# Low parts of weights made a layer ahead, memory values as split products, and a planner that goes backwards and forwards

## The chip, the cores and the metric

The kernel runs on one core of one Trainium2 chip. The metric is the device time of one execution in microseconds (us), smaller is better; a median of several runs is compared. A profile is one execution taken by the hardware profiler: it lists each instruction of TensorE (PE for its matmuls, PEld for its weight loads), VectorE (DVE), ScalarE (ACT), GpSimd (POOL), and SyncE (SP), which only issues DMAs here. GpSimd issues DMAs too, on a queue of its own.

## The reference

One inference step of a two-layer streaming encoder, in fp32, for 384 tokens of width 1024: 8 running streams of 16 tokens (128) and one new stream of 256. Layer 0 mixes tokens by a Conformer convolution, layer 1 by a gated deltanet:

```python
h = rms_norm(x, P['norm_pre'][i, 0])
f = swiglu(h, ...);  x = x + 0.5 * rms_norm(f, P['norm_post'][i, 0])
h = rms_norm(x, P['norm_pre'][i, 1])
y = conformer_conv_module(h, ...) if i % 2 == 0 else gated_deltanet(h, ...)
x = x + rms_norm(y, P['norm_post'][i, 1])
h = rms_norm(x, P['norm_pre'][i, 2])
a = memory_cross_attention(h, mem_k[i], mem_v[i], ...)
x = x + rms_norm(a, P['norm_post'][i, 2])
h = rms_norm(x, P['norm_pre'][i, 3])
f = swiglu(h, ...);  x = x + 0.5 * rms_norm(f, P['norm_post'][i, 3])
```

`swiglu` is `(silu(h @ w_gate) * (h @ w_up)) @ w_down` with an inner width of 2816. The convolution module is a 1024 to 2048 projection, a gate (`val * sigmoid(gate)`), a depthwise convolution of 31 taps, a layer norm with silu, and a 1024 to 1024 projection with bias. For the new stream, memory keys and values are outputs, and needed by the cross-attention of each layer:

```python
p_mem_k = jnp.einsum('bmd,lde->lbme', mem_prompt, xa_wk)   # 256 memory tokens, 2 layers
p_mem_v = jnp.einsum('bmd,lde->lbme', mem_prompt, xa_wv)
```

The running streams bring theirs in a cache.

## The kernel before

**Split products.** An fp32 weight chunk of 128 x 1024 numbers (512 KB) is loaded into one of three `raw` buffers (SP), cast by ScalarE to a rounded type, fp32r, as its high part `whi`, and DVE subtracts to get the low part `wlo` (`Emitter.get`, L289 and after; the subtraction is L197's, the cast L189's). High and low parts lie in a ring of eight buffers each: chunk j takes buffer j % 8, and `done` frees it in the program's order. Activations are split likewise (`hTh`, `hTl`; `rbh`, `rbl`). A product is then three fp32r matmuls: high x high, high x low, low x high. All matmuls are issued at L247 (`mm`), transposes at L279.

**Kinds of products.** `gmm` makes 128 output features for all 384 tokens: 8 k-steps x 3 matmuls of 384 columns. `dmm` adds one k-step of a down projection: for 128 tokens and each half of 512 output columns 3 matmuls. `wide` is a projection of 512 features with tokens as rows.

**Stages in order.** Start (three norm chains), feed-forward block of layer 0 (`ffn(0, 0)`), convolution (`conv`), cross-attention (`xattn(0)`), feed-forward (`ffn(0, 1)`), then for layer 1 feed-forward, `deltanet`, `xattn(1)`, feed-forward. A feed-forward block has 22 passes f: a gate chunk, an up chunk, and the down chunk of an earlier pass, so 48 matmuls of 384 columns and 18 of 512. At the end of each stage `tokenwise` finishes three groups of 128 tokens in turn, each followed by a `chain`: the sum of squares on ScalarE, a power on GpSimd (`rstd`), the residual on DVE, transposes, and the next split.

**The convolution.** Eight pairs of input chunks (`cg`, `cv`); each pair's result is gated (`glu`: GpSimd clears the left padding, ScalarE and DVE make the product and copy a window). DVE then applies 31 taps per feature chunk (`taps`, L210), two chunks at a time; taps that meet only cached rows are done in the block before (`old_taps`). PE adds up the mean, `ln` normalises on DVE, ScalarE, PE and GpSimd, and eight output chunks (`co`, all eight weight buffers) with a bias chunk (`bout`, split into spare columns of `rbh` and `rbl`) finish it.

**Memory keys and values.** `kv(n)` emits n units, taken from a list: for both kinds, 2 layers, 4 heads and 2 feature halves, 32 units in all. A unit loads 512 KB of weights as plain fp32 into a slot (four slots beside the memory itself, in `big`), does 16 fp32 matmuls of 128 columns, copies the result on ScalarE, and GpSimd stores it. The units have no successors in their stage, so they fill PE's idle time; the table `KV` says how many are emitted where (start 3, first block 3, convolution 20, its output 3, then 1 and 2).

**What sets the order.** The program is emitted once into a list of operations, each with a cost from a formula (`act`, `tt`, `ts`, `mm`, ...). `Scheduler.graph` finds dependencies from the parts of the tiles that are read and written. `Scheduler.order` then simulates: each of the five engines takes, whenever it is free, the ready operation with the longest path of costs to the end, plus a bonus given by hand. DMAs go through one pipe of 360 bytes per ns, eight in flight per queue. The instructions of each engine are issued in the order found, and each engine works strictly through its own.

## Time and profile before

| | us |
|---|---|
| median of 3 runs | 1885.33 |
| lowest and highest | 1884.56, 1886.7 |
| the profiled execution | 1886.81 |
| its span, first to last instruction | 1885.0 |

The profiled execution had a granted clock of 0.999. About 1.8 us of its time lies around its span. "Busy" counts an engine's instructions alone; a DMA's time to landing runs from its issue to the arrival of its last byte.

### The profile page before, as it was taken

The numbers are of one execution on the slowest core, as the hardware profiler recorded it, in microseconds if no ns is written. First come the engines' busy times: TensorE is split into PE (matmuls) and PEld (weight loads), VectorE is DVE, ScalarE is ACT, GpSimd is POOL, SyncE is SP. The second block draws the span as 40 slices with busy tenths as digits, with TensorE's granted clock in tenths as the row PEclk, the third lists the DMA queues.
The fourth block names the chain that finished last, engine by engine and source line by source line (L and its number), as shares of the span: only waits on it lengthen the run. The fifth ranks groups of instructions, "written<-read, shape, count | busy, mean of one in ns | idle before, by whom it ended". The sixth has DMA issues, their size and how long they took to land.

```text
span 1885.0 us, 27534 instructions
## 1 busy us (share of the span) xinstructions
PE 1860.1 (99%) x10895; PEld 1682.0 (89%) x10895; DVE 1011.6 (54%) x1708; ACT 753.8 (40%) x1435; POOL 170.2 (9%) x391
## 2 busy tenths in 40 slices
PE   8999999999999999999999999999999999999998
PEld 8999999999877899999899999999998766899997
DVE  6564436999553633333633333688776734533333
ACT  4333334312643632333433233676564534432332
POOL 1000002111100100000100000323221101000000
PEclk9999999999999999999999999999999999999999
DMA  8543434556686534434434333323325682444331
GB/s 303 178 136 126 134 112 122 127 147 219 213 314 216 157 123 134 132 125 130 154 115 131 123 124 111 118 79 116 126 93 165 228 316 74 137 132 135 123 123 45
DMA packets 88466, 278.81 MB, mean 148 GB/s; under 512 B 18001, under 2 KB 20561, under 8 KB 88337
## 3 DMA queue, kind: packets, MB, share of 16 engines
q1 hardware_dynamic: 86080, 271.42, 44.8%
q0 software_dynamic: 2256, 5.64, 0.9%
q8 instruction: 85, 1.39, 0.3%
q14 instruction: 45, 0.36, 0.1%
HBM read 265.09 MB, written 11.92 MB: 147 GB/s over the span
## 4 chain that ended last, share of the span: by engine, by line
PE 94%; DVE 1%; DMA 1%; ACT 1%; POOL 1%; issue 1%; SPq 0%; DVEq 0%; POOLq 0%; ACTq 0%
PE ps L247 89%; PE ps L279 3%; PE ps L259 2%; POOL stat L197 1%; DVE big L210 1%; ACT big L190 1%; DMA big<-in_cv 0%; DMA x<-in_x 0%; DMA raw<-in_w 0%; PE ps L272 0%; DVE big L197 0%; ACT hTl L190 0%; ACT whi L189 0%; DMA big<-in_state 0%; DVE wlo L197 0%
## 5 line engine op out<-in xcount | busy, mean ns | idle before, releaser
L197 DVE TENSOR_TENSOR wlo<-raw,whi 128x1024 fp32r<-128x1024 f32 x361 | 438.6, 1222 | 581.4 <-ACT whi L189 555.7
L189 ACT CAST whi<-raw 128x1024 fp32r<-128x1024 f32 x361 | 374.5, 1051 | 652.5 <-PE ps L247 603.5
L247 PE MATMUL ps<-hTh,wlo 128*128 128x384 f32 x1680 | 495.4, 339 | 0.0
L247 PE MATMUL ps<-hTh,whi 128*128 128x384 f32 (+1 forms) x1680 | 494.5, 340 | 0.1
L247 PE MATMUL ps<-hTl,whi 128*128 128x384 f32 x1680 | 493.8, 340 | 0.0
L247 PEld LDWEIGHTS ps<-hTh,whi 128*128 128x128 f32 x1680 | 308.7, 188 | 8.0 <-ACT big L190 1.0
L247 PEld LDWEIGHTS ps<-hTl,whi 128*128 128x128 f32 x1680 | 308.8, 188 | 6.9 <-issue 1.5
L247 PEld LDWEIGHTS ps<-hTh,wlo 128*128 128x128 f32 x1680 | 309.0, 188 | 4.2 <-issue 0.4
L247 PE MATMUL ps<-big 128*128 128x128 f32 (+3 forms) x1912 | 283.7, 286 | 9.9 <-DMA big<-in_w 6.4
L247 PEld LDWEIGHTS ps<-big 128*128 128x128 f32 x1912 | 256.7, 193 | 35.0 <-issue 17.8
L247 PE MATMUL ps<-whi,rbh 128*128 128x512 f32 x672 | 205.2, 396 | 0.4 <-DVE big L210 0.4
L247 PE MATMUL ps<-wlo,rbh 128*128 128x512 f32 x672 | 203.0, 395 | 0.0
L247 PE MATMUL ps<-whi,rbl 128*128 128x512 f32 x672 | 201.7, 394 | 0.0
L210 DVE SCALAR_TENSOR_TENSOR big<-big,cols 128x384 f32<-128x384 f32 (+13 forms) x424 | 189.3, 499 | 2.6 <-ACT big L190 0.3
L247 PEld LDWEIGHTS ps<-whi,rbl 128*128 128x128 f32 x672 | 125.7, 188 | 24.8 <-issue 0.4
L247 PEld LDWEIGHTS ps<-wlo,rbh 128*128 128x128 f32 x672 | 125.3, 188 | 24.6 <-issue 0.8
L247 PEld LDWEIGHTS ps<-whi,rbh 128*128 128x128 f32 x672 | 124.9, 188 | 20.5 <-DVE big L210 0.6
L279 PE MATMUL ps<-ident,big 128*128 128x128 f32 x479 | 86.0, 275 | 6.0 <-DVE big L210 5.6
L247 PE MATMUL ps<-whi,hTh 128*128 128x512 f32 x240 | 87.7, 401 | 0.2 <-ACT hTh L189 0.2
L197 DVE TENSOR_TENSOR big<-big,ps 128x384 f32<-128x384 f32 (+4 forms) x131 | 67.2, 519 | 36.2 <-PE ps L247 36.1
L247 PE MATMUL ps<-whi,hTl 128*128 128x512 f32 x240 | 86.4, 398 | 0.1
L204 POOL TENSOR_SCALAR stat<-stat 128x1 f32<-128x1 f32 (+2 forms) x48 | 16.8, 350 | 767.6 <-ACT hTl L190 754.0
(84 smaller groups left out, 1337.8 us busy)
## 6 DMA issues: line engine op xcount, KB each, us to landing
raw<-in_w SPq DMA_DIRECT2D x362, 512.0 KB, 3.7
big<-in_w SPq DMA_DIRECT2D x37, 512.0 KB, 4.7
big<-in_ck SPq DMA_DIRECT2D x32, 512.0 KB, 6.3
big<-in_cv SPq DMA_DIRECT2D x32, 512.0 KB, 6.6
big<-in_npre SPq DMA_DIRECT2D x8, 512.0 KB, 7.5
big<-in_npost SPq DMA_DIRECT2D x8, 512.0 KB, 6.2
out_pkv<-big POOLq DMA_DIRECT2D x32, 128.0 KB, 5.1
big<-out_pkv SPq DMA_DIRECT2D x8, 512.0 KB, 6.3
```

The source lines that it names most:

```text
L189: return self._on("A", cost, dep, lambda: sc.copy(out, in_), [in_], w)
L190: return self._on("A", cost, dep, lambda: sc.activation(out, in_, func, **kw), [in_, bias, scale] + ([] if after is None else [after]), w, ...
L197: return self._on(eng, cost, dep, lambda: e.tensor_tensor(out=out, in0=a, in1=b, op=op), [a, b], [out])
L204: return self._on(eng, cost, dep, lambda: e.tensor_scalar(out=out, in0=a, scalar1=s1, scalar2=s2, op0=op0, **kw), [a, s1, s2 if s2 is not ...
L210: lambda: v.scalar_tensor_tensor(out=out, in0=a, scalar=s, in1=b, op0=op0, op1=op1), [a, s, b], [out])
L247: self._add("P", cost, lambda: t.matmul(out, lhsT, rhs, start=start, stop=stop, **kw), [lhsT, rhs], [out])
L259: t.matmul(out, lhsT, rhs, start=start, stop=stop)
L279: self._add("P", 109.0, lambda: t.transpose(out, in_, ident), [in_, ident], [out])
```

## The change

**Values as split products.** The value weights become 16 chunks `("v4", layer, half of 512 columns, quarter of k)`. A new function, emitted after the convolution's input chunks, splits the memory (two chunks, into columns of `rbh` and `rbl` that the bias does not use) and multiplies; the list of `kv` keeps the 16 key units, each now 8 fp32 matmuls of 256 columns:

```diff
+    def kv_split(self):
...
+        for i in range(2):
+            c = slice(i * D, (i + 1) * D)
+            E.get(("mem", i), dest=(mh[:, c], ml[:, c]))
...
+        for l in range(2):
+            for u in range(2):
+
+                (o, b) = self.bank2()
+                for q in range(4):
+                    j, wh, wl = E.get(("v4", l, u, q))
+                    for k in range(2 * q, 2 * q + 2):
+                        s = slice(512 * (k % 2), 512 * (k % 2) + 512)
+                        for m in range(2):
+                            c = slice(m * P, (m + 1) * P)
+                            E.mm(o[m], mh[:, k, c], wh[:, s], k == 0, False)
+                            E.mm(o[m], mh[:, k, c], wl[:, s], False, False)
+                            E.mm(o[m], ml[:, k, c], wh[:, s], False, k == KT - 1)
+                            E.pump()
+                    E.done(j)
+                for m in range(2):
+                    r = result(o[m], 512)
+                    for n in range(2):
+                        E.store(self.O["pkv"][l, 2 * u + n][:, 512 + m * MEM:512 + (m + 1) * MEM],
+                                r[:, n * MEM:(n + 1) * MEM])
...
-            for m in range(2):
-                c = slice(m * P, (m + 1) * P)
-                for k in range(KT):
-                    a, b_ = (w[:, k, :], mem[:, k, c]) if kind == "wk" else (mem[:, k, c], w[:, k, :])
-                    E.mm(o[:, c], a, b_, k == 0, k == KT - 1)
+            for k in range(KT):
+                E.mm(o[:, 0:MEM], w[:, k, :], mem[:, k, :], k == 0, k == KT - 1)
...
-KV = {"start": 3, "f00": 3, "conv": 20, "co": 3, "xo": 0, "f01": 1, "f10": 2, "dn": 6, "f11": 0}
+KV = {"start": 3, "f00": 3, "conv": 5, "co": 2, "xo": 0, "f01": 1, "f10": 2, "dn": 0, "f11": 0}
-SLOTS = 4
+SLOTS = 3
```

**Low parts made ahead.** 35 chunks, those of the convolution's last four input pairs, the memory, the values, the bias and the output projection, are split once more than needed, two in each pass f = 3 to 20 of the first feed-forward block: loaded, cast, subtracted, and the low part stored in DRAM by GpSimd. When the chunk is needed, its high part is made as before, and its low part is loaded by GpSimd's queue into the weight buffer; the subtraction goes.

```diff
+AHEAD = [(n, k) for k in range(4, KT) for n in ("cg", "cv")] + [("mem", 0), ("mem", 1)]
+AHEAD += [("v4", l, u, q) for l in range(2) for u in range(2) for q in range(4)] + [("bout",)] + [("co", k) for k in range(KT)]
...
         self.load(raw, self.wall[CHUNK[name]])
         self.act(hi, raw)
-        self.tt(lo, raw, hi.bitcast(F32), ALU.subtract)
+        if name in self.low:
+            self.store(lo, self.low.pop(name))
+        else:
+            self.tt(lo, raw, hi.bitcast(F32), ALU.subtract)
         return j, hi, lo
+
+    def ahead(self, name):
+
+        j, hi, lo = self.get(name)
+        self.low[name] = self.scr[self.nlow]
+        self.nlow += 1
+        self.store(self.low[name], lo)
+        self.done(j)
...
+            if (l, i) == (0, 0) and f >= FIRST_AHEAD:
+
+                for n in AHEAD[2 * (f - FIRST_AHEAD):2 * (f - FIRST_AHEAD) + 2]:
+                    E.ahead(n)
```

**The planner.** The costs take other figures (a split matmul of n columns is set at (n + 32) / 2.4 + 1.2 ns instead of n / 2.4 + 3, and GpSimd's powers, copies and sums at a little more than before). The forward simulation is now `early`; `late` runs the same simulation from the end backwards and gives each operation a latest time. The first plan is the old one (longest path plus bonus); three times, a backward run on the last plan gives the ranks of a new forward run, and a plan with an earlier end by the planner's own figures replaces the one kept. Input chunk c of the convolution gets a bonus of -12000 c in the first plan.

```diff
+        at, self.end = self.early([o.path + o.bonus for o in ops])
+        new = at
+        for _ in range(PASSES):
+            new, end = self.early(self.late(new, pred))
+            if end < self.end:
+                at, self.end = new, end
+        for i, o in enumerate(ops):
+            o.at = at[i]
+        self.final = [ops[i] for i in sorted(range(len(ops)), key=lambda i: (at[i], i))]
         return self.final
```

More of the change, by code (lines that the diff above doesn't have):

```diff
@@ L47 @@
 TAIL = 3
+PASSES = 3
+POOLTRUE = 1
 LANES = 8
@@ L105, in __init__ @@
         self.names = []
-        self.dest = {}
+        self.low, self.nlow = {}, 0
         self.bonus = 0.0
@@ L201, in ts @@
         r = 1.05 if self._ps(a) else 0.525
-        cost = 65 + r * self._n(out) if eng == "V" else 260 + 3.6 * self._n(out)
+        cost = 65 + r * self._n(out) if eng == "V" else 305 + 3.6 * self._n(out)
         kw = {} if op1 is None else {"op1": op1}
@@ L240, in mm @@
         if rhs.dtype == F32R:
-            cost = max(107.0, n / 2.4) + 3
+            cost = max(60.0, (n + 32) / 2.4 + 1.2)
         else:
-            cost = 2 * max(107.0, n / 1.2) + 2
+            cost = 2 * max(111.0, n / 1.2 + 2.5)
         self.vt += cost
@@ L252, in quad @@
         n = self._n(mms[0][2])
-        cost = 2 * max(107.0, n / 1.2) + 85.0
+        cost = 2 * max(107.0, n / 1.2) + 190.0
         self.vt += cost
@@ L265, in strips @@
         n = self._n(mms[0][2])
-        cost = 2 * max(107.0, n / 1.2) + 170.0
+        cost = 2 * max(107.0, n / 1.2) + 260.0
         self.vt += cost
@@ L394, in lat, with late, pick, early @@
         return self.LAT[o.eng].get(p.eng, 150)
-    def order(self):
+    def late(self, at, pred):
         ops = self.ops
-        self.graph()
-        for o in reversed(ops):
-            o.path = o.cost + max((self.lat(o, ops[j]) + ops[j].path for j in o.succ), default=0.0)
+        nsucc = [len(o.succ) for o in ops]
+        rd, res = [0.0] * len(ops), [0.0] * len(ops)
         free = dict.fromkeys("PAVGS", 0.0)
         now, later = {e: [] for e in free}, {e: [] for e in free}
-        dma = 0.0
+        for i, o in enumerate(ops):
+            if not o.succ:
+                heapq.heappush(later[o.eng], (0.0, i))
+        for _ in ops:
+            best, e, i = self.pick(free, now, later, lambda i: -at[i] - ops[i].cost)
+            o = ops[i]
+            res[i] = free[e] = best + o.cost
+            for j in pred[i]:
+                rd[j] = max(rd[j], res[i] + self.lat(ops[j], o))
+                nsucc[j] -= 1
+                if not nsucc[j]:
+                    heapq.heappush(later[ops[j].eng], (rd[j], j))
+        return res
+    @staticmethod
+    def pick(free, now, later, key):
+        best, e = None, None
+        for f in free:
+            if now[f]:
+                t = free[f]
+            elif later[f]:
+                t = max(free[f], later[f][0][0])
+            else:
+                continue
+            if best is None or t < best:
+                best, e = t, f
+        while later[e] and later[e][0][0] <= best:
+            i = heapq.heappop(later[e])[1]
+            heapq.heappush(now[e], (key(i), i))
+        return best, e, heapq.heappop(now[e])[1]
+    def early(self, prio):
+        ops = self.ops
+        npred = [o.npred for o in ops]
+        rd, at = [0.0] * len(ops), [0.0] * len(ops)
+        free = dict.fromkeys("PAVGS", 0.0)
+        now, later = {e: [] for e in free}, {e: [] for e in free}
+        dma, last = 0.0, 0.0
         table = None
@@ L408, in order @@
                 heapq.heappush(later[o.eng], (0.0, i))
-        out = []
-        for _ in range(len(ops)):
-            best, be = None, None
-            for e in free:
-                if now[e]:
-                    t = free[e]
-                elif later[e]:
-                    t = max(free[e], later[e][0][0])
-                else:
-                    continue
-                if best is None or t < best:
-                    best, be = t, e
-            e = be
-            while later[e] and later[e][0][0] <= best:
-                _, i = heapq.heappop(later[e])
-                heapq.heappush(now[e], (-ops[i].path - ops[i].bonus, i))
-            _, i = heapq.heappop(now[e])
+        for _ in ops:
+            best, e, i = self.pick(free, now, later, lambda i: -prio[i])
             o = ops[i]
@@ L437, in order @@
                 dma = max(dma, end + DMA_IN) + o.nbytes / 360.0
-                fin = dma + DMA_OUT
-                lane.append(fin)
-                del lane[0]
-            out.append(i)
+                end = dma + DMA_OUT
+                lanes[e] = lanes[e][1:] + [end]
+            last = max(last, end)
             for j in o.succ:
-                s = ops[j]
-                s.ready = max(s.ready, fin if o.nbytes else end + self.LAT[e].get(s.eng, 150))
-                s.npred -= 1
-                if not s.npred:
-                    heapq.heappush(later[s.eng], (s.ready, j))
-        self.end = max(free.values())
-        self.final = [ops[i] for i in sorted(out, key=lambda i: (ops[i].at, i))]
+                rd[j] = max(rd[j], end + (0.0 if o.nbytes else self.LAT[e].get(ops[j].eng, 150)))
+                npred[j] -= 1
+                if not npred[j]:
+                    heapq.heappush(later[ops[j].eng], (rd[j], j))
+        return at, last
+    def order(self):
+        ops = self.ops
+        self.graph()
+        pred = [[] for _ in ops]
+        for i, o in enumerate(ops):
+            for j in o.succ:
+                pred[j].append(i)
+        for o in reversed(ops):
+            o.path = o.cost + max((self.lat(o, ops[j]) + ops[j].path for j in o.succ), default=0.0)
+        at, self.end = self.early([o.path + o.bonus for o in ops])
[4 more added lines that the diff above has]
+                at, self.end = new, end
+        for i, o in enumerate(ops):
+            o.at = at[i]
+        self.final = [ops[i] for i in sorted(range(len(ops)), key=lambda i: (at[i], i))]
         return self.final
```

57 lines of the change are left out of this document (38 added, 19 removed).

## The prediction

> **What bounds the kernel now.** I read the page first: engine totals and the chain that ended last.
>
> ```profile
> span 1885.0 us, 27534 instructions
> PE 1860.1 (99%) x10895; PEld 1682.0 (89%) x10895; DVE 1011.6 (54%) x1708; ACT 753.8 (40%) x1435; POOL 170.2 (9%) x391
> PE 94%; DVE 1%; DMA 1%; ACT 1%; POOL 1%; issue 1%; SPq 0%; DVEq 0%; POOLq 0%; ACTq 0%
> ```
>
> TensorE is the bound, but "99%" is a mean over stages. So next came the busy time by stretch (columns: stretch, length, then PE, PEld, DVE, ACT, POOL busy with instruction counts, granted clock, DMA share, GB/s).
>
> ```profile
> 0.00:20.00 20.00, 12.72 (x82) 11.97 (x83) 4.12 (x6) 7.41 (x18) 3.88 (x17) 1.00 0.90 335
> 100.00:150.00 50.00, 50.00 (x266) 46.88 (x266) 34.71 (x80) 15.80 (x20) 0.00 (x0) 1.00 0.42 133
> 350.00:400.00 50.00, 50.00 (x353) 50.00 (x352) 48.31 (x115) 13.79 (x21) 12.04 (x19) 1.00 0.51 114
> 400.00:450.00 50.00, 50.00 (x439) 49.21 (x438) 50.00 (x100) 4.86 (x13) 8.40 (x13) 1.00 0.60 182
> 450.00:500.00 50.00, 49.57 (x306) 43.31 (x305) 30.09 (x36) 27.30 (x52) 8.04 (x14) 1.00 0.71 257
> 500.00:550.00 50.00, 50.00 (x319) 37.97 (x318) 31.86 (x44) 26.63 (x49) 6.32 (x10) 1.00 0.72 252
> 1180.00:1240.00 60.00, 58.22 (x417) 56.82 (x416) 45.47 (x100) 44.02 (x96) 22.26 (x54) 1.00 0.34 110
> 1440.00:1640.00 200.00, 192.76 (x1127) 147.52 (x1126) 101.29 (x166) 87.10 (x196) 19.20 (x38) 0.99 0.56 188
> 1880.00:1885.00 5.00, 0.00 (x0) 0.00 (x0) 1.41 (x2) 0.00 (x0) 0.15 (x1) 0.79 0.47 176
> ```
>
> Three facts matter. In the first feed-forward block (100 to 150 us) PE never rests, and vector engine, ScalarE and DMA are at most 70% used. In the convolution (350 to 450) PE never rests either, yet DVE is full too (98 of 100 us): here two engines are the bound at once. PE's few idle microseconds lie at the start (7.3), the end (5) and from 1180 to 1640, in the deltanet and second cross-attention. The third view, the chain in order of time, agrees for the convolution: one piece of PE work from 312 to 464.
>
> ```profile
> 312.07 152.25 PE ps L247 x1116
> ```
>
> So work taken off PE in the convolution is worth its own length, if DVE's stretch there shrinks as well and nothing added starves PE.
>
> **Part 1: memory values, on PE.** The pace of a matmul is the distance between starts, not its recorded length. The rows are a stretch of filler passes alone (fp32, 128 columns); two fp32 passes of 256 columns that are two starts apart; two split passes (fp32r, 512 columns) that are eight apart; and two stores of memory units with 13 units from one to the other.
>
> ```profile
> 405.00:411.00 6.00, 6.00 (x56) 1.00 0.87 253
> 570.18 0.38 PE L247 MATMUL ps<-big 128*128 128x256 f32 x1
> 570.61 0.38 PE L247 MATMUL ps<-big 128*128 128x256 f32 x1
> 482.03 0.39 PE L247 MATMUL ps<-whi,hTl 128*128 128x512 f32 x1
> 483.84 0.39 PE L247 MATMUL ps<-whi,hTh 128*128 128x512 f32 x1
> 405.16 0.73 POOL L286 DMA_DIRECT2D out_pkv<-big  x1 [5.33 <-ACT big L189]
> 452.86 0.56 POOL L286 DMA_DIRECT2D out_pkv<-big  x1 [4.37 <-ACT big L189]
> ```
>
> 6 us over 54 to 56 passes is 0.110 us each. The stores show that a unit, 16 fp32 matmuls in the code, takes two such passes per matmul: 47.7 / 13 = 3.67 us with some matmuls of the mean between, against 32 x 0.110 = 3.52, which I take. An fp32 pass of 256 columns takes 0.43 / 2 = 0.215, a split pass of 512 takes 1.81 / 8 = 0.226.
>
> - Values before: 16 units x 3.52 = 56.3 us. After: 2 layers x 2 column halves x 8 k x 2 row halves x 3 products = 192 passes x 0.226 = 43.4. Gain 12.9.
> - Keys: 16 units, now 16 passes of 256 columns each, 16 x 0.215 = 3.44 instead of 3.52. Gain 1.3.
>
> Together 14.2 us. By place: convolution and its output projection held 20 + 3 units, 81.0 us, and will hold 5 + 2 key units and the values, 24.1 + 43.4 = 67.5, so 13.5 of the gain falls there.
>
> **Part 2: low parts ahead, off DVE.** DVE in the convolution: first tap, first and last weight subtraction among the taps, the unbroken run of taps, the bias's subtraction after the last tap; then the first output matmul on PE.
>
> ```profile
> 324.58 0.41 DVE L204 TENSOR_SCALAR big<-big,cols 128x256 f32<-128x256 f32 x1
> 329.65 1.23 DVE L197 TENSOR_TENSOR wlo<-raw,whi 128x1024 fp32r<-128x1024 f32 x1 [0.21 <-ACT whi L189]
> 363.78 1.22 DVE L197 TENSOR_TENSOR wlo<-raw,whi 128x1024 fp32r<-128x1024 f32 x1
> 397.89 56.04 DVE L210 SCALAR_TENSOR_TENSOR big<-big,cols 128x238 f32<-128x238 f32 x111
> 453.85 1.22 DVE L197 TENSOR_TENSOR rbl<-raw,rbh 128x1024 fp32r<-128x1024 f32 x1
> 476.23 0.48 PE L247 MATMUL ps<-whi,hTh 128*128 128x512 f32 x1
> L197 DVE TENSOR_TENSOR wlo<-raw,whi 128x1024 fp32r<-128x1024 f32 x361 | 438.6, 1222 | 581.4 <-ACT whi L189 555.7
> L189 ACT CAST whi<-raw 128x1024 fp32r<-128x1024 f32 x361 | 374.5, 1051 | 652.5 <-PE ps L247 603.5
> ```
>
> Seven subtractions of the last eight input chunks lie among the taps: 7 x 1.2 = 8.4 us off a run from 324.6 to 453.9. The bias's and the eight output chunks' subtractions lie in and behind the layer norm that follows (453.9 to 476.2); of their 9 x 1.2 I count 3 to 5 us as in the way of that chain. DVE would reach the first output matmul 11.5 to 13.5 us earlier, PE 13.5 earlier. Neither is left far behind, so the stage ends about 13 us sooner, 12 after the 1 us that Part 4 takes; had DVE only its 8.4, it would be 8.4. ScalarE keeps all casts; value results are eight copies of 512 columns, cheap on an engine with 4.86 of 50 us busy.
>
> **Part 3: what is put into the first block.** 35 chunks, two in each of 18 passes (f = 3 to 20): per chunk a load of 512 KB, a cast (1.05), a subtraction (1.22), a store of 512 KB. A pass is 66 matmuls; 266 in 50 us make it 12.4 us. Casts and subtractions come to 2.1 and 2.4 us per pass and fit into the idle time of both engines; their cover is PE's 12.4 us. What may not fit is the ring of three raw buffers, which now serves five chunks per pass instead of three. A buffer is taken for the landing, the cast and the subtraction, L + 2.3 us; three buffers serve five chunks in 12.4 us as long as L is below 3 x 12.4 / 5 - 2.3 = 5.1 us. Landings (the page's medians in KB and us; then min/median/max of weight loads between 500 and 600 us, and between 450 and 500; last a stretch that shows DMA's ceiling):
>
> ```profile
> raw<-in_w SPq DMA_DIRECT2D x362, 512.0 KB, 3.7
> out_pkv<-big POOLq DMA_DIRECT2D x32, 128.0 KB, 5.1
> out_sconv<-big POOLq DMA_DIRECT2D x8, 120.0 KB, 7.0
> DMA to landing us min/median/max: 3.4/4.4/8.6
> DMA to landing us min/median/max: 3.5/5.8/7.3
> 12.00:24.00 12.00, 11.10 (x96) 10.83 (x96) 8.08 (x12) 9.08 (x22) 3.90 (x8) 1.00 1.03 407
> ```
>
> Traffic rises from 133 GB/s by four transfers of 524,288 bytes per 12.4 us, 169 GB/s, to about 300, against a ceiling of 407. At 252 GB/s the median was 4.4, at 257 it was 5.8. With 4.4 the block costs nothing; with 5.8 a pass takes 5 x 8.1 / 3 = 13.5, and 18 passes lose 20 us. I take 4.4 to 5, no loss, since the 4.4 stretch is the longer one and feeds the same ring beside other 512 KB loads, and keep 20 for the range. Those stores leave by another queue than the loads. If that kept them apart, L would stay at 3.7; the rows say that landings grow with the total. The Trainium skill says the same and against this change: in DMA: Bandwidth & Descriptors, under "Issuing engines are not separate DMA queues", transfers run on the same 16 engines and interleave whichever engine issued them. By that rule too, the loss is 0 at a landing of 4.4 and 20 at 5.8, where separate queues would make it 0 for certain; the trace agrees.
>
> **Part 4: what is put on GpSimd's queue.** 35 stores, then 35 loads of low parts, each issued in about 0.56 to 0.73 us (the two rows of Part 1, under a full DVE), 70 x 0.7 = 49 us of an engine busy 9%. The new wait: a load of a low part waits, on GpSimd, for PE to leave its weight buffer, and behind it stand the convolution's padding memsets, its stores and the layer norm's powers. DVE and ScalarE wait for those. The plan orders them by expected time, so a wait costs only what PE lags the plan; I put it at 0 to 3 us and take 1. A buffer then turns in about 8 us (0.7 plus 5 to 7), against 8 buffers x 12 passes x 0.226 = 22 us for the values. Traffic in the convolution grows by 35 x 0.52 MB over some 150 us, by 122 GB/s on 114 to 257: 236 to 379, the upper end near the ceiling, but only around the output chunks.
>
> **Part 5: order and small edits.** New duration figures cost nothing themselves; they and the backward and forward passes move instructions. Elsewhere PE is full, so only 1180 to 1640 can move. The waits of weight loads there (total, times, longest):
>
> ```profile
> PEld ps L247 <- issue: 14.0, 32, 1.6
> PEld ps L279 <- DVE big L210: 5.7, 5, 3.5
> ```
>
> The long ones (5.7) and PE's idle 1.8 + 7.2 are what a better order can remove: 0 to 10; a worse one can add as much. I take 3, nearer to none because the waits are scattered in serial chains. One slot less for memory weights (three units, 10 us of PE work, still lie ahead of each load), memory loaded once more (1 MB, 2.6 us at 407 GB/s if PE did not cover it) and the rank of the input chunks: nothing, hidden by full PE.
>
> **Sum.** The profiled execution took 1886.8 us (span 1885.0 and 1.8 around it), 1.5 above the median. 1886.8 - 12 (convolution) - 0.7 (keys elsewhere) - 3 (order) = 1871.1; less 1.5, **1869.6, say 1869**.
>
> **Rivals.**
>
> - **Raw ring (slower).** Landings in the first block pass 5.1 us and the ring, no longer PE, sets its pace. For it: 300 GB/s lies above the stretch that had 5.8. Against: loads there came in bursts, here they are even. At 5.8: 1869 + 20 = 1889; at 6.2, 1901.
> - **Order loses.** Waits between 1180 and 1640 grow by 10 instead of shrinking by 3: 1882. For it: the serial heads leave PE thin there; against: durations now match the pace shown above.
> - **Order wins more.** All 10 us of long waits go, and some of the 14 of "issue": 1869 - 7 to - 17, about 1857. Against: most waits are short.
> - **DVE alone sets the convolution.** Only 8.4 of 12 is gained: 1873; with GpSimd's queue late by 3, 1876.
> - **The new passes find no better plan** and the first order stands: 1872.
>
> **How the numbers follow.** Forecast with the last two, 1863 to 1877: 0.65. Order wins more: 0.13. Order loses: 0.10. Raw ring: 0.12. This kernel's measurement tells about 0.2% (3.8 us) from no change, 1881.6 to 1889.1. Faster 0.80, same 0.09, slower 0.11. The range of 1853 to 1885 leaves out the ring's case and the far end of the order's gain.
>
> **What would show it.** Right: value passes fp32r and 512 wide, about 192 at 0.226; the first output matmul of the convolution at 464 instead of 476; the first block ending at the same time as before (convolution's first split pass still near 312); 17 to 18 fewer subtractions between 322 and 480. Wrong: ScalarE's casts in the first block waiting for raw loads with medians over 5.1; PE idle before 300; GpSimd's issue rows with long waits for PE followed by late powers; or stretches from 1180 on that shift by more than 10 us.

## The result and the profile after

The change makes the kernel slower by 0.8%: 1900.70 us (median of 4, 1899.44 to 1902.60) against 1885.20 before, a ratio of 1.0079 (95% interval 1.0066 to 1.0092). The forecast was 1869, the range ended at 1885. The profiled execution took 1901.28 us, its span 1899.5. First the page after: span, engine totals, granted clock by fortieths, and the two DMA queues (packets, MB, share of 16 engines).

```profile
span 1899.5 us, 26738 instructions
PE 1857.4 (98%) x10319; PEld 1651.3 (87%) x10319; DVE 1033.4 (54%) x1726; ACT 805.0 (42%) x1478; POOL 206.8 (11%) x461
...
PEclk9999999999999999999999999999999999999999
DMA  8788875879678344343444334323334592543431
...
q1 hardware_dynamic: 91408, 290.82, 46.9%
q0 software_dynamic: 12336, 42.34, 6.3%
```

PE has 576 matmuls fewer, as the change says, and is "98%" busy instead of 99%, in a span 14.5 us longer. The DMA row shows where to look: 5 to 9 in the first 13 slices (617 us), 3 or 4 in most of those behind them.

Where the time went is read from PE's timeline, by the same instruction in both traces: the first split matmul of the first block and of the convolution, the first output matmul of the convolution, the deltanet's first split matmul of 384 columns, and one of 384 columns soon after the last block's first.

| stage (us) | before | after | difference |
|---|---|---|---|
| start | 23.1 | 21.8 | -1.3 |
| first feed-forward block | 289.2 | 307.0 | +17.8 |
| convolution, to its first output matmul | 164.0 | 166.7 | +2.7 |
| output, cross-attention, two feed-forward blocks | 718.5 | 720.9 | +2.4 |
| deltanet and second cross-attention | 444.6 | 437.3 | -7.3 |
| last block and end | 245.6 | 245.8 | +0.2 |

So two things are to be explained: 17.8 us lost where I had put nothing, and 12 us that the convolution was to give and didn't. Deltanet and second cross-attention gave more than the 3 us that I had put there.

**The first block.** Busy time by stretch (columns as in the prediction), then what engines waited for from 24 to 312 us (total, times, longest), then ScalarE's timeline and PE's one row with a wait from 49 to 58 us:

```profile
24.00:60.00 36.00, 31.68 (x168) 30.21 (x167) 27.95 (x50) 16.39 (x20) 1.43 (x3) 0.94 0.85 272
60.00:200.00 140.00, 137.37 (x713) 127.08 (x712) 97.13 (x163) 63.52 (x74) 10.66 (x20) 0.99 0.82 273
200.00:320.00 120.00, 114.93 (x585) 103.56 (x584) 62.76 (x68) 54.78 (x78) 12.69 (x28) 1.00 0.73 241
```

```profile
ACT whi L196 <- DMA raw<-in_w: 137.2, 80, 8.3
...
PEld ps L254 <- ACT big L197: 10.4, 9, 4.8
...
PE ps L254 <- ACT big L197: 7.1, 4, 4.3
```

```profile
50.36 1.05 ACT L196 CAST whi<-raw 128x1024 fp32r<-128x1024 f32 x1 [2.51 <-DMA raw<-in_w]
51.63 1.05 ACT L196 CAST whi<-raw 128x1024 fp32r<-128x1024 f32 x1 [0.22 <-DMA raw<-in_w]
55.89 1.05 ACT L196 CAST whi<-raw 128x1024 fp32r<-128x1024 f32 x1 [3.20 <-DMA raw<-in_w]
56.84 0.48 ACT L197 ACTIVATE big<-ps 128x384 f32<-128x384 f32 x1
```

```profile
57.38 0.69 PE L254 MATMUL ps<-hTh,whi 128*128 128x384 f32 x1 [4.32 <-ACT big L197]
```

(Lines have shifted: casts are L196, subtractions L204, silu L197, taps L217, matmuls L254, loads L290, GpSimd's transfers L293.) PE stopped at 53.06 and waits 4.32 us for the silu at 56.84, which frees the PSUM bank (one of the accumulators that matmuls write) that it wants. ScalarE doesn't idle before the silu (no bracket in its row); the silu stands in ScalarE's order behind the cast at 55.89, and that one waits for its raw buffer to land. In these three stretches PE is idle for 12.0 us (their lengths less its busy time), 7.1 of them for the silu. Behind the waits the granted clock is 0.50 from 56.0 to 62.7 and from 322.2 to 325.6 us, which takes some 5 us of PE work more (an estimate: half of 10.1). Together that is near the 17.8 lost.

Worked out over 83 chunks issued from 60 to 290 us, a raw buffer's turn is 4.94 us of landing, 0.45 to the cast, 1.05 cast, 0.31 to the subtraction, 1.22 subtraction, 0.03 to the next issue: 8.0, so 2.67 us per chunk, where 12.4 / 5 = 2.48 is wanted. Before, the same sum was 12.45, of which 6.0 is a landed buffer that waits to be cast: the ring had slack. The ring's pace alone would make a pass 5 x 2.67 = 13.4 us and cost 18 passes 17 us, nearly the loss. The experiments show that this agreement is chance.

**The convolution.** The last taps and what follows on DVE, and the first output matmul; then DMA from 400 to 490 us (GB/s in 40 parts, then issues: count, KB, median us to landing):

```profile
450.73 11.37 DVE L217 SCALAR_TENSOR_TENSOR big<-big,cols 128x384 f32<-128x384 f32 x18
476.58 3.48 DVE L204 TENSOR_TENSOR big<-big,ps 128x1024 f32<-128x1024 f32 x3 [14.49 <-PE ps L254]
```

```profile
495.50 0.39 PE L254 MATMUL ps<-whi,hTh 128*128 128x512 f32 x1
```

```profile
GB/s 401 351 20 64 231 75 218 399 409 411 408 404 399 171 162 280 411 408 408 405 221 267 246 397 410 404 419 282 133 248 364 408 410 410 402 408 393 391 402 222
...
raw<-in_w SPq DMA_DIRECT2D x21, 512.0 KB, 8.2
wlo<-scr_lo POOLq DMA_DIRECT2D x18, 512.0 KB, 9.0
big<-in_w SPq DMA_DIRECT2D x5, 512.0 KB, 12.8
```

The same view of the kernel before, 420 to 460 us:

```profile
big<-in_w SPq DMA_DIRECT2D x9, 512.0 KB, 4.1
...
raw<-in_w SPq DMA_DIRECT2D x2, 512.0 KB, 6.1
```

DVE does what was forecast: its taps end 462.1 - 328.8 = 133.3 us after the stage's start, before 453.9 - 312.3 = 141.6, 8.3 us sooner. Then it waits 14.49 us for PE, which has yet to add up the mean, and the first output matmul comes 33.4 us after the last tap instead of 22.3. DMA stands at 390 to 420 GB/s in more than half of these parts, and a weight load lands in 8 to 13 us instead of 4 to 6. What GpSimd, PE's weight loads and PE waited for from 329 to 496 us, and PE's two rows with a wait behind its last value pass:

```profile
POOL wlo L293 <- PE ps L254: 53.1, 22, 10.1
...
PEld ps L254 <- DMA wlo<-scr_lo: 9.1, 8, 2.3
...
PE ps L254 <- DMA wlo<-scr_lo: 6.2, 6, 1.9
```

```profile
468.73 1.02 PE L254 MATMUL ps<-big 128*128 128x256 f32 x2 [2.09 <-DMA big<-in_w]
470.42 11.80 PE L254 MATMUL ps<-big 128*128 128x256 f32 x48 [0.67 <-DMA big<-in_w]
```

GpSimd waits for PE to leave a weight buffer before it issues a low part's load, and PE waits in turn for such loads. When the last tap ends at 462.1, PE is still at the values; a key unit that waits for its weights comes next, and the last pass of the mean (fp32, 384 columns) stands behind that unit and starts at 476.06, 14 us after the tap. Before, it started at 456.44, 2.5 us after the last tap.

To put numbers on PE's standing still, I count each matmul at its pace (0.226 us for 512 columns and the fp32 paces of the prediction, 0.174 for a split pass of 384) and take that from a stage's length. First block: before 1.6, after 22.9. Convolution: before 1.8, after 15.9. From the first split pass to the end: before 59, after 90. These 31 us more, less 14.2 us of work and 1.3 at the start, come to 15.5, near the 14.5 that the span grew.

### The profile page after: what moved, and what is told of

It reads as the page before. It is cut to its first block, busy times and chain, and to the rows that moved or that the text cites. A ratio compares the mean times of both kernels' runs of the same rounds, so it can differ in the third digit from the quotient of the medians.

```text
span 1899.5 us, 26738 instructions
## 1 busy us (share of the span) xinstructions
PE 1857.4 (98%) x10319; PEld 1651.3 (87%) x10319; DVE 1033.4 (54%) x1726; ACT 805.0 (42%) x1478; POOL 206.8 (11%) x461
## 5 line engine op out<-in xcount | busy, mean ns | idle before, releaser
L204 DVE TENSOR_TENSOR wlo<-raw,whi 128x1024 fp32r<-128x1024 f32 x380 | 462.3, 1223 | 533.8 <-ACT whi L196 526.5
L196 ACT CAST whi<-raw 128x1024 fp32r<-128x1024 f32 x412 | 431.5, 1051 | 701.0 <-PE ps L254 472.5
L254 PE MATMUL ps<-hTh,whi 128*128 128x384 f32 (+1 forms) x1680 | 513.9, 341 | 9.5 <-ACT big L197 7.9
L254 PE MATMUL ps<-hTl,whi 128*128 128x384 f32 (+1 forms) x1680 | 510.3, 339 | 0.0
L254 PE MATMUL ps<-hTh,wlo 128*128 128x384 f32 x1680 | 504.1, 338 | 0.0
L254 PEld LDWEIGHTS ps<-hTh,whi 128*128 128x128 f32 x1680 | 310.3, 188 | 23.6 <-ACT big L197 12.6
L254 PEld LDWEIGHTS ps<-hTl,whi 128*128 128x128 f32 x1680 | 310.8, 188 | 9.0 <-issue 2.0
L254 PEld LDWEIGHTS ps<-hTh,wlo 128*128 128x128 f32 x1680 | 310.0, 188 | 4.8 <-issue 0.3
L254 PE MATMUL ps<-wlo,rbh 128*128 128x512 f32 x736 | 230.7, 397 | 6.9 <-DMA wlo<-scr_lo 6.2
L254 PE MATMUL ps<-whi,rbh 128*128 128x512 f32 x736 | 234.0, 399 | 1.7 <-ACT whi L196 1.7
L254 PE MATMUL ps<-big 128*128 128x256 f32 (+3 forms) x1144 | 219.6, 320 | 10.5 <-DMA big<-in_w 9.5
L254 PE MATMUL ps<-whi,rbl 128*128 128x512 f32 x736 | 228.9, 395 | 0.0
L254 PEld LDWEIGHTS ps<-big 128*128 128x128 f32 x1144 | 179.8, 193 | 41.3 <-issue 13.5
L217 DVE SCALAR_TENSOR_TENSOR big<-big,cols 128x384 f32<-128x384 f32 (+12 forms) x424 | 191.9, 504 | 3.1 <-POOL big L222 0.2
L254 PEld LDWEIGHTS ps<-wlo,rbh 128*128 128x128 f32 x736 | 138.5, 189 | 38.1 <-DMA wlo<-scr_lo 9.1
L254 PEld LDWEIGHTS ps<-whi,rbh 128*128 128x128 f32 x736 | 137.1, 188 | 27.2 <-ACT whi L196 2.8
L254 PEld LDWEIGHTS ps<-whi,rbl 128*128 128x128 f32 x736 | 137.5, 188 | 25.9 <-issue 0.4
L204 DVE TENSOR_TENSOR big<-big,ps 128x384 f32<-128x384 f32 (+4 forms) x131 | 67.5, 521 | 91.1 <-PE ps L254 78.7
L211 POOL TENSOR_SCALAR stat<-stat 128x1 f32<-128x1 f32 (+2 forms) x48 | 16.5, 343 | 772.8 <-ACT hTl L197 753.3
L254 PE MATMUL ps<-whi,hTh 128*128 128x512 f32 x240 | 85.6, 399 | 0.5 <-ACT hTh L196 0.5
L254 PE MATMUL ps<-whi,hTl 128*128 128x512 f32 x240 | 84.9, 399 | 0.8 <-DVE hTl L204 0.8
```

What stands on the lines that cost most here:

```text
L196: return self._on("A", cost, dep, lambda: sc.copy(out, in_), [in_], w)
L204: return self._on(eng, cost, dep, lambda: e.tensor_tensor(out=out, in0=a, in1=b, op=op), [a, b], [out])
L211: return self._on(eng, cost, dep, lambda: e.tensor_scalar(out=out, in0=a, scalar1=s1, scalar2=s2, op0=op0, **kw), [a, s1, s2 if s2 is not ...
L217: lambda: v.scalar_tensor_tensor(out=out, in0=a, scalar=s, in1=b, op0=op0, op1=op1), [a, s, b], [out])
L254: self._add("P", cost, lambda: t.matmul(out, lhsT, rhs, start=start, stop=stop, **kw), [lhsT, rhs], [out])
```

## The experiments

Theory A: the loads, casts and stores made ahead, and the loads of low parts, make queues wait; B: the new order loses. Of A there are three forms in the first block: **ring** (three raw buffers turn too slowly), **queue** (casts stand too early in ScalarE's order), **stores** (they hold the weight buffers). Lengths in us; "next" is output, cross-attention and two feed-forward blocks; the ratio is to runs of the kernel before on the same chip (medians 1885.2 to 1886.6). Times are medians where there is a ratio; the lengths come from one profiled execution each. Runs of one kernel that loads more than before differ by up to 11 us (plan_late 1880.4 to 1891.9, lo_given 1878.0 to 1887.1), so a difference of a few us in one length, or between single runs, shows nothing by itself.

| run | time | ratio (95%) | first block | convolution | next | deltanet, 2nd cross-attention |
|---|---|---|---|---|---|---|
| before | 1885.2 | | 289.2 | 164.0 | 718.5 | 444.6 |
| after | 1900.7 | 1.0066 to 1.0092 | 307.0 | 166.7 | 720.9 | 437.3 |
| no_ahead | 1915.1 | 1.0139 to 1.0169 | 287.4 | 196.5 | 722.1 | 439.3 |
| order_only | 1888.5 | 0.9999 to 1.0018 | 289.8 | 165.3 | 723.5 | 438.5 |
| old_order | 1904.2 | 1.0079 to 1.0113 | 305.2 | 164.7 | 722.9 | 440.5 |
| made_unused | 1938.5 | 1.0259 to 1.0290 | 311.4 | 197.7 | 721.8 | 438.6 |
| mk_loadonly | 1923.9 | one run | 299.2 | 194.5 | 722.2 | 438.8 |
| mk_noload | 1935.8 | one run | 303.6 | 197.6 | 723.1 | 438.5 |
| raw4 | 1909.9 | 1.0093 to 1.0137 | 307.4 | 162.2 | 727.5 | 434.5 |
| fewer | 1910.7 | 1.0116 to 1.0146 | 310.4 | 169.7 | 721.0 | 439.1 |
| plan_late | 1886.8 | 0.9985 to 1.0011 | 292.2 | 160.8 | 721.4 | 439.6 |
| plan4 | 1889.9 | 1.0008 to 1.0028 | 288.3 | 162.7 | 721.8 | 446.0 |
| plan_first4 | 1886.0 | 0.9989 to 1.0007 | 292.3 | 166.8 | 721.2 | 437.5 |
| order_late | 1884.2 | 0.9979 to 0.9997 | 287.5 | 162.1 | 724.3 | 438.8 |
| lo_given | 1883.4 | 0.9967 to 0.9990 | 287.4 | 161.8 | 722.9 | 439.7 |
| v_nolow | 1883.5 | one run | 289.4 | 160.1 | 725.8 | 439.1 |
| spread | 1894.9 | 1.0026 to 1.0052 | 290.0 | 175.3 | 720.5 | 438.8 |
| lo_plan | 1880.9 | one run | 286.3 | 164.2 | 721.1 | 437.2 |
| nokeys | 1895.8 | one run | 287.2 | 157.2 | 723.3 | 456.2 |
| v_held | 1876.0 | one run | 286.6 | 160.8 | 720.7 | 438.4 |

### Which part costs: making, use, or order

**no_ahead**: split values and new planner, nothing made ahead.

```diff
-            if (l, i) == (0, 0) and f >= FIRST_AHEAD:
+            if False:
```

> Split values and the new planner stay; nothing is made ahead, DVE makes every low part when it is due (18 more subtractions in the convolution than before, 22 us of DVE). Theory A, that the loads, casts and stores put into the first block cost it its 17.8 us: the first split pass of the convolution is back at 312 to 315 (after 328.8, before 312.3). DVE, full in the convolution, gets 22 us more: first output matmul 170 to 186 us behind the first split pass (before 163.9, after 166.7). Total 1885 + 6 to 22 - 8 from the deltanet on = 1883 to 1899. Theory B, that the new order costs the block: the first split pass still at 322 or later, total 1900 or more.

The first block is back at 287.4: A holds. The convolution grows by 32.5, more than the 22 us of subtractions and than I expected: PE stands with the mean at the head of its order and waits for taps. Its waits in the whole convolution, 26.0 of these 28.4 us between 350 and 410, and then the busy time of that stretch:

```profile
PE ps L254 <- DVE big L217: 28.4, 4, 15.7
```

```profile
350.00:410.00 60.00, 32.56 (x147) 28.17 (x146) 60.00 (x130) 7.62 (x11) 6.27 (x9) 0.77 0.23 49
```

DVE is full and PE nearly half idle. So split values without low parts made ahead cost more than they bring: 1915.1 us.

**order_only**: the kernel before with the new figures, `late`, `early` and `order`, and nothing else of the change. **old_order**: after with the old figures and the first plan.

```diff
-PASSES = 3
+PASSES = 0
```

> The kernel before with the new duration figures and the backward and forward passes alone. Theory A: the first block keeps its 312 within 3, the convolution its 164 within 4, and the 7.7 us that deltanet and second cross-attention gained come from the order and show here: 1876 to 1882. Theory B (the order loses in the first block or the convolution): first split pass at 320 or later, or the convolution over 170; total 1890 or more.

> The whole change, but with the old duration figures and only the first plan. Theory A: the first block still ends at 325 or later (the same loads and stores pass through the same three buffers), the convolution does not get shorter than 164, and the 7.7 us from deltanet to second cross-attention are gone: 1900 to 1912. Theory B: the first block ends at 312 to 315 and the total is 1882 or less.

Deltanet and second cross-attention show the new order's gain in order_only (444.6 to 438.5), but 5.0 us are lost in "next" and 1.3 in the convolution: no measurable difference in all, between A's 1876 to 1882 and B's 1890 or more. With the old order the first block keeps 305.2 and the convolution 164.7, as A expects; B falls, as the cause of either loss. Of the 7.3 us won from the deltanet on, 3.2 go without the new planner; whether order or work brings the others isn't separated.

**made_unused**: made and stored, never read.

```diff
-        if name in self.low:
-            self.store(lo, self.low.pop(name))
+        if False:
+            pass
```

> After, but the low parts made and stored in the first block are never read; DVE subtracts in the convolution as before, 18 subtractions more for memory and values. Theory A: the first block ends at 325 to 332 as in after. In the convolution the queue of GpSimd holds no loads and the traffic falls by 18 MB: if the loads of low parts were what kept PE and DVE apart there, the waits of PE for the low parts vanish, and DVE's 22 us more of subtractions set its length: 170 to 186, total 1899 to 1915. If the first block's loss were the order's, it would end near 312 here as well.

The first block loses 22.2 us with no use of what it makes. The convolution is as long as in no_ahead, so this run says nothing on the loads there. My expectation for the total was 23 us too low, half of it in the convolution.

### What it is in the first block

**mk_loadonly** keeps of each chunk made ahead only its load; **mk_noload** all but its load (both from made_unused); **raw4** is after with four raw buffers.

```diff
-        j, hi, lo = self.get(name)
...
+        self.load(self.raw[self.nraw % RAW], self.wall[CHUNK[name]])
+        self.nraw += 1
```

```diff
-        self.load(raw, self.wall[CHUNK[name]])
+        if load:
+            self.load(raw, self.wall[CHUNK[name]])
...
-        j, hi, lo = self.get(name)
+        j, hi, lo = self.get(name, load=False)
```

```diff
-RAW = 3
+RAW = 4
-BIG = 17300
+BIG = 16276
```

> Of the 35 chunks made ahead in the first block only the loads into the three raw buffers are left: no cast, subtraction, store or weight buffer; nothing of it is used, DVE subtracts in the convolution. Read at the first split pass of the convolution (312 without the making, 333 with all of it but no use). If the loads' traffic and the raw buffers by themselves cost the block (ring): 322 or later. If the cost is that casts and subtractions stand in the order of ScalarE and DVE ahead of the gate's work and wait there (queue), or that stores hold the weight buffers (stores): 312 to 316.

> The 35 chunks are cast, subtracted and stored in the first block as in the run with the making unused, but without their loads: each takes what lies in its raw buffer. 0.5 MB less per chunk, and the casts wait for no load of their own. Ring or queue: the first split pass of the convolution at 312 to 317. Stores, or the weight buffers held by them, or the plain work of ScalarE and DVE: 322 or later.

> After with four raw buffers instead of three (the tile big is 1024 columns smaller). Four buffers serve five chunks per 12.4 us as long as a landing takes less than 4 x 12.4 / 5 - 2.3 = 7.6 us; the medians were 4.6 to 4.8. Ring: the first block ends at 312 to 317, the convolution unchanged, total 1884 to 1890. Queue: casts are placed by the plan, which knows shorter landings than the chip; a fourth buffer lets the loads start earlier and helps in part, 316 to 324, total 1888 to 1896. Stores: no change, 326 to 331, total 1896 to 1903.

No one form expected all three. mk_noload (first split pass of the convolution at 329.4) and raw4 (331.0) came out where the stores form had them, but mk_loadonly, which has no added stores, still loses, to 321.0, between its two cases. Loads alone cost 10 to 12 us; everything but the loads costs 14 to 16; together 17.8 to 24. Four buffers bring nothing in the first block (307.4), though now a landed buffer waits 2.27 us on average for its cast, so the ring has slack again. The ring as the cause falls; stores fall with plan_late, which keeps them all.

**fewer**: 26 chunks ahead (bias and output projection subtracted when due) over the same 18 passes. **plan_late**: after with one figure of the planner changed, the time from a transfer's last byte to its use.

```diff
-AHEAD += [("v4", l, u, q) for l in range(2) for u in range(2) for q in range(4)] + [("bout",)] + [("co", k) for k in range(KT)]
+AHEAD += [("v4", l, u, q) for l in range(2) for u in range(2) for q in range(4)]
```

```diff
-DMA_IN, DMA_OUT = 650.0, 950.0
+DMA_IN, DMA_OUT = 650.0, 2600.0
```

> After, with 26 chunks made ahead instead of 35 (bias and output projection are subtracted again when due), one or two in each of the same 18 passes: 4.44 chunks per pass, so a raw buffer may take 3 x 12.4 / 4.44 = 8.4 us against the 8.0 measured. Ring theory: the first block loses 0 to 6 us instead of 17.8 (ends at 312 to 318). Queue theory: about 26 / 35 of the loss, 13 us, ends at 324 to 327. The convolution has 9 subtractions more behind the taps, 3 to 5 us in the way, and 4.7 MB less to load: 163 to 170. Total 1884 to 1892 by the ring, 1893 to 1900 by the queue.

> After, but the planner reckons with 1.65 us more from a transfer's end to its use (a 512 KB load then lands 4.7 us after its issue, as measured in the first block of after, instead of 3.1). Nothing that is done changes, only the order of the queues. In after a raw buffer turned in 8.0 us on average (landing 4.94, 0.45 to the cast, cast 1.05, 0.31 to the subtraction, subtraction 1.22), 2.67 us per chunk where 12.4 / 5 = 2.48 is wanted. Queue theory (ScalarE's casts stand too early in its order and hold up the gate's work): the first block ends at 313 to 320, total 1885 to 1893. Ring theory (three buffers are too slow in whatever order): 325 to 331, total 1896 to 1903.

fewer missed on both counts (310.4 with less to make, 1910.7 in all): the loss isn't proportional to the bytes, and the ring is slack here too (a landed buffer waits some 2.2 us for its cast). plan_late did what the queue form expects in both numbers: it gives 14.8 us back in the first block and 13.9 in all, and its raw buffers turn in 8.03 us, as in after (8.00). ScalarE's and PE's waits from 24 to 312 us, then ScalarE from 51 to 55 us:

```profile
ACT whi L196 <- DMA raw<-in_w: 96.8, 71, 3.9
...
PEld ps L254 <- DVE wlo L204: 4.3, 6, 0.9
```

```profile
51.38 1.05 ACT L196 CAST whi<-raw 128x1024 fp32r<-128x1024 f32 x1 [1.52 <-DMA raw<-in_w]
52.88 0.49 ACT L197 ACTIVATE big<-ps 128x384 f32<-128x384 f32 x1 [0.45 <-PE ps L254]
53.90 1.05 ACT L196 CAST whi<-raw 128x1024 fp32r<-128x1024 f32 x1 [0.52 <-DMA raw<-in_w]
```

The waits of PE and of its weight loads for the silu (7.1 and 10.4 us in after) are gone; at the place shown, the silu now stands ahead of the cast that waits. That is the queue form, shown: same work, same buffers, same turn, another order. PE's waits for the silu are also there in every other run that loses 10 us or more in this block (6.9 to 12.3 us in made_unused, mk_loadonly, mk_noload, raw4, fewer and old_order), and there are none in the kernel before.

**plan4** and **plan_first4** add a fourth raw buffer to plan_late, throughout or in the first block alone (taken from `big`):

```diff
+        if (l, i) == (0, 0):
+            more, moreh = self.alloc(D)
+            E.ring = E.raw + [more]
```

> After with the longer landings in the plan and four raw buffers. Queue theory: once the plan knows the landings, the fourth buffer takes the rest of the first block's loss (3 us) and part of the convolution's waits: 1876 to 1885. If buffers never mattered, as four of them alone brought nothing: within 3 us of plan_late's 1886.8.

> After with the longer landings in the plan and a fourth raw buffer in the first block alone, taken from the tile big and given back, so that nothing is smaller later. First block 288 as with four buffers throughout (292 with three), the rest as in plan_late: 1886.8 - 4 = 1883, 1880 to 1886. If the fourth buffer's gain there was chance: 1886 to 1890.

With four buffers throughout the first block is whole (288.3), but 6.4 us more are spent from the deltanet on than in plan_late; with four in that block alone it is 292.3, no better than three. In that run PE waits 5.5 us for the silu again, so what a buffer brings hangs on the order that the planner finds with it. Both expectations of a gain failed: that a fourth buffer helps isn't shown.

**order_late** is order_only with the same figure.

> The kernel before with the new planner and its longer landings, no other change. The planner alone gave 1.0008 of before: 7 us won from the deltanet to the second cross-attention and as much lost elsewhere. If the loss elsewhere comes from plans that trust short landings, this keeps the 7: 1877 to 1882. If not: 1884 to 1890.

1884.2, the second case: 4.3 us less than order_only, and the one version that leaves out nothing of the computation and whose whole interval lies below the kernel before, by 2.4 us, which is inside what I called no difference. The gain of 7 is not kept whole: "next" takes 5.8.

### What it is in the convolution

**lo_given** makes nothing and loads, as low parts, the weights themselves: first block clean, convolution's traffic that of after.

```diff
-        j, hi, lo = self.get(name)
...
+        self.low[name] = self.wall[CHUNK[name]].bitcast(F32R)
```

> After, but nothing is made in the first block: what is loaded as a low part in the convolution comes from the weights themselves (so the low parts are wrong, the traffic of the convolution is that of after). First block at 312. If the convolution's loss lies in its own loads of low parts (18 MB more through GpSimd's queue) or in the order: it keeps 163 to 169 us, and the total is 1881 to 1886. If it was only dragged by the late first block (the taps of cached rows, the clock): 150 to 157 us, total 1868 to 1874, which is what I forecast for the whole change.

161.8, 1883.4 in all: nearest the first case. Even given for nothing, the change brings 2.2 us there, not 12; DVE's taps end 131.0 us after the start (before 141.6), PE stands still for 12.3. DMA share and GB/s (last two columns) while PE is at the values:

```profile
390.00:410.00 20.00, 18.49 (x79) 14.35 (x79) 20.00 (x46) 7.05 (x8) 6.94 (x13) 1.00 1.05 327
410.00:430.00 20.00, 17.60 (x76) 13.87 (x75) 20.00 (x47) 7.44 (x9) 6.67 (x12) 1.00 1.04 292
430.00:450.00 20.00, 17.70 (x76) 14.50 (x75) 10.14 (x18) 8.07 (x12) 7.58 (x14) 0.95 1.06 345
```

Four runs from lo_given take single suspects away. **v_nolow** loads no low parts of values, **spread** emits the values in four parts among the input pairs, **lo_plan** has the longer landings, **nokeys** has `"conv": 0, "co": 0` in `KV`.

```diff
         if name in self.low:
+            if name[0] == "v4":
+                return j, hi, hi
```

```diff
+            if c % 2:
+                next(values, None)
...
-        self.kv_split()
```

> The run with given low parts, without the 16 loads of the values' low parts (the high part is taken twice, so the values are wrong): 8.4 MB less in the convolution, the same work on PE, ScalarE and DVE. While PE works on values there, a chunk of 12 x 0.226 = 2.7 us needs 1.05 MB, 387 GB/s, and DMA was full (1.04 to 1.06 at 292 to 345 GB/s from 390 to 450). If that traffic is what kept the convolution at 162 us: 150 to 156 now, and PE's waits for low parts gone. If the order is to blame (key units ahead of the mean): 159 to 163.

> The run with given low parts, with the value products emitted in four parts, after the input pairs 1, 3, 5 and 7, instead of all after pair 7. Same work, same traffic, evenly laid: 40 MB over the convolution's 155 us is 258 GB/s. Traffic theory: convolution 150 to 157 us instead of 161.8, total 1872 to 1879. If the waits come from anything else (GpSimd's queue, the order of the means): 159 us or more, total 1880 to 1886.

> The run with given low parts (nothing made in the first block, low parts wrong, convolution 161.8 us of which PE stands still for 11) with a planner that reckons with landings 1.65 us longer. If PE's waits in the convolution come from a plan that trusts too short landings: its stalls between 350 and 450 fall below 4 us and the convolution takes 150 to 156, span 1868 to 1874. If three raw buffers are too slow for the values whatever the order (2.7 us per chunk wanted, 2.7 or more given): stalls stay at 8 to 12, the convolution at 159 to 163.

> The run with given low parts, with the seven key units of the convolution and its output moved to the cross-attentions (24 us of PE work, and 3.7 MB, out of the convolution). If PE's work plus its waits set the convolution's length: DVE's taps end as before at 440 and the first output matmul comes 22 us behind them as in the kernel before, 462, so the convolution is 152 to 155. If it is the mean's place in PE's order behind values that wait: 158 or more. The units must then fit elsewhere: up to 24 us later where PE is full, less in deltanet and second cross-attention, where it has idle time.

None reaches the 150 to 157 that its suspect would have explained: 160.1, 175.3, 164.2 and 157.2, with PE still for 11.5, 25.8, 13.8 and 25. Each time another wait comes up at the head of PE's order: in spread one key unit that waits 10.1 us for its weights, in nokeys the bias matmuls, which wait 4.8 us for a PSUM bank of the values' results. nokeys also shows that moved filler isn't free: 16.5 us come back later.

**v_held** takes the whole supply of value chunks away: no load, cast or low part, same matmuls.

```diff
+        if name[0] == "v4":
+            return j, hi, lo
         self.load(raw, self.wall[CHUNK[name]])
```

> The run with given low parts, in which the 16 chunks of value weights are neither loaded nor cast nor given a low part: PE multiplies with what lies in its weight buffers (values wrong, low parts wrong). PE's work is the same, DVE's too. If the supply of the value chunks (landing, raw buffer, cast, low part) makes PE stand still for 12 us in the convolution: at most 4 us are left and the convolution takes 150 to 156. If the other waits of the filler do (key weights, PSUM banks that wait for results to be copied and stored, the mean behind them): 8 us or more are left, 158 to 162.

By stretch (busy time), then two rows of PE at the end of the values, then issues from 420 to 450 us:

```profile
311.00:430.00 119.00, 119.00 (x609) 108.78 (x608) 111.04 (x244) 27.81 (x38) 24.24 (x42) 1.00 0.48 136
430.00:436.00 6.00, 6.00 (x29) 5.03 (x28) 5.59 (x11) 2.79 (x5) 3.05 (x5) 1.00 1.06 399
436.00:447.00 11.00, 4.51 (x13) 2.90 (x12) 7.49 (x13) 2.32 (x4) 3.82 (x7) 0.78 1.06 258
```

```profile
436.59 0.39 PE L254 MATMUL ps<-whi,rbl 128*128 128x512 f32 x1
442.52 1.19 PE L254 MATMUL ps<-big 128*128 128x256 f32 x2 [5.54 <-DMA big<-in_w]
```

```profile
wlo<-in_w POOLq DMA_DIRECT2D x7, 512.0 KB, 12.7
raw<-in_w SPq DMA_DIRECT2D x6, 512.0 KB, 11.8
big<-in_w SPq DMA_DIRECT2D x3, 512.0 KB, 15.4
```

For 125 us PE doesn't stop: the supply of the value chunks did cause the waits spread over 350 to 430. Then it waits 5.54 and 0.95 us for key weights and works at a granted clock of 0.50 behind that, some 10 us lost by the count at its pace, and the convolution is 160.8, one us less than with the supply. The output projection's weights, their low parts and three key loads are all under way at 399 GB/s, a key load lands in 15.4 us, and the mean stands behind that unit. So the second half of my either-or came true as well: one wait took the place of the other. Common to both is a DMA share of 1.04 or more where PE waits. But in v_held the share was only 0.48, at 136 GB/s, for 119 us before, and the three key loads were issued at 428 to 432 us: this last wait is one of order, not of bytes alone. What stays open is whether a better order at after's traffic could hold the 150 to 156; no order that I tried did.

## Why the prediction was wrong, point by point

- **Part 1** (value passes, 14.2 us of PE work) held: 576 matmuls fewer, and value passes 0.226 us apart in v_held, with PE never idle for 125 us. The gain in work is there and is eaten by waits.
- **Part 2**, DVE's 8.4 us: measured 8.3. But "Neither is left far behind, so the stage ends about 13 us sooner" is the step that failed in the convolution: from the last tap to the first output matmul it took 33.4 us instead of 22.3, as PE, late by its waits, had the mean behind filler.
- **Part 3**, "I take 4.4 to 5, no loss", is the step that failed first, by 17.8 us. Two errors. The bound of 5.1 left no time for a buffer to wait in the queues of ScalarE and DVE: landing 4.94 plus 0.45 and 0.31 is 5.7, beyond it. And what a late load costs isn't the ring's pace: casts that wait hold up the silu behind them in ScalarE's order. The raw ring rival named the right place; its mechanism fell with raw4, fewer and plan_late. That its 20 us at a landing of 5.8 come near the 17.8 lost at 4.94, and its 1889 to 1901 near the 1900.7, is luck: the total holds 12 us of the convolution that the rival still had as won.
- **Part 4**: "the upper end near the ceiling, but only around the output chunks" was mis-sized. I spread 18 MB over 150 us; a value chunk asks for 1.05 MB per 12 x 0.226 = 2.7 us, 387 GB/s, for as long as PE is at values. And "A buffer then turns in about 8 us" took landings of 5 to 7: in the loaded queue it is 9.0 us from issue to landing alone, after waits of GpSimd for PE (53.1 us in 22 times). Against the 1 us that I took stand some 11: 161.8 in lo_given, where 152 was forecast with that 1 in it. How much of it is traffic and how much order isn't separated.
- **Part 5**: -3 in all was wrong, the place right: deltanet and second cross-attention gained 6.1 by the order alone, of the 10 that I had bounded. "Elsewhere PE is full, so only 1180 to 1640 can move" was wrong: a full PE can still lose, and in order_only's one profile it lost 6.9.
- The signs that I named for "wrong" came: casts that wait for raw loads in the first block, PE idle before 300, and GpSimd's long waits for PE in the convolution. Only the median of the landings, 4.7 from 60 to 300 us, stayed under its 5.1; it hides the long ones, up to 7.9.

## What to carry to other kernels

When engines work through a fixed order, the price of a late transfer is what stands behind the instruction that waits for it, not the transfer's length; put the measured landing under the new load into the plan (here one figure, 1.65 us, was worth 14 of the 15.5 us that the change had lost, and still no gain). Cost added traffic by the stretch in which it falls, bytes over the time of the work that needs them, and ask whether that stretch, not the stage, stays under the ceiling. Where PE is full, work taken away is only a gain if every filler that is left can run without waiting.

## What the runs showed of the hardware

Transfers from both queues together stop at 400 to 426 GB/s (after 400 to 490 us, v_held 420 to 450 us, by fortieths), and landings of 512 KB grow from 3.7 us to 8 to 15 there. The Trainium skill, DMA: Bandwidth & Descriptors, section "Specifications", gives 435 GB/s as the fabric's ceiling; the traces end a few per cent below it.

A wait of PE costs more than its length. Three stretches behind a wait, of 4.32 and 2.09 us in after and of 5.54 us in v_held; the third number from the end is the granted clock:

```profile
56.00:62.70 6.70, 5.32 (x14) 4.67 (x15) 3.47 (x4) 2.88 (x4) 0.00 (x0) 0.50 0.75 263
469.00:475.80 6.80, 6.13 (x15) 4.36 (x15) 0.00 (x0) 0.68 (x2) 1.10 (x2) 0.50 1.07 411
442.20:448.90 6.70, 5.43 (x12) 3.96 (x13) 1.64 (x3) 0.59 (x1) 1.63 (x3) 0.50 1.05 381
```

At that clock split passes of 384 columns start 0.32 us apart (no_ahead, 382 to 385 us) instead of 0.174. The Trainium skill, TensorE: Matmul & The Clock Gate, section "What's actually happening", halves the clock after an idle window of about 3.4 us. The waits of 4.32 and 5.54 us agree; the one of 2.09 us is shorter than such a window and was followed by the same clock, so here less than 3.4 us of standing still was enough, though not every time: in lo_given, with a wait of 2.1 us from 413.3 us on, the clock from 410 to 430 us was 1.00.
